# Nineteen weight tiles in the ring instead of seventeen, second weights stored by pairs of row blocks, and a smaller DMA scratch

## The chip, the cores and the metric

The kernel runs on one core of a Trainium2 chip, in one launch. The metric is the device time of an execution in microseconds. The engines are TensorE (PE; its weight loads are PEld), VectorE (DVE), ScalarE (ACT), GpSimd (POOL) and SyncE (SP), which here issues nearly all transfers. Each engine works through its own instructions in order; semaphores hold them until data has come or a buffer is free.

## The reference

Two transformer blocks run over 256 tokens of width 1024, all in fp32. What matters here is the first block's expert layer and the shapes of the rest:

```python
# block 1: a mixer (causal convolution of 31 taps, attention of 8 heads with forget gates, gates), then
def moe_ffn(h, w_router, b_router, w1, b1, w2, b2):      # 32 experts, the best 4 for each token
    logits = hf @ w_router + b_router
    top_v, top_e = lax.top_k(logits, TOP_K)
    gates = softmax(top_v)
    ...
    hc = xi @ w1[e] + b1[e]                              # 1024 -> 2048
    g, u = min(hc[:, :1024], 7), clip(hc[:, 1024:], -7, 7)
    hm = (u + 1) * (g * sigmoid(1.702 * g))
    yb = hm @ w2[e] + b2[e]                              # 1024 -> 1024
    y = sum over a token's four experts of gate * yb
# block 2: mixer(0), a feed-forward layer of 22 x 128 hidden columns, mixer(1),
#          then a second expert layer: 8 experts, 11 x 128 hidden columns, the best 2 for each token
```

The first expert layer alone reads 32 x (8 + 4) MiB of weights; the whole kernel reads 694 MB.

## The kernel before, in words

The stages of one execution, with their places in the profile: the first mixer (0 to 255 us), the first expert layer (255 to 1220), a normalisation and mixer(0) (1220 to 1437), the feed-forward (1437 to 1630), mixer(1) (1630 to 1825) and the second expert layer (1825 to the end).

**Weights and the ring.** Every weight tile is 128 partitions of 2048 fp32 numbers (1 MiB). `load` (line 245, its transfer is issued on line 247) takes the next tile of a ring and has SyncE start the transfer. A pool of seven tiles, `ring`, lives through the whole kernel. While a stage has room left, `more_ring` names a second pool and an order: a letter "m" is a tile of that pool, a letter "r" one of the seven. In the first expert layer the order is `RING1` with 17 letters, ten "m" and seven "r"; in the second it is "rrrrrrrm", eight. A tile is written again when the products that read it are done, so the load of one tile waits on the products that used the tile 17 loads before.

**The first expert layer.** For each of 32 experts eight tiles of first weights (`in_wei`, a block of 128 rows of 8 KB each) and four of second weights (`in_weo`, two blocks of 128 rows of 4 KB each) are loaded, in that order. The number of tokens that an expert has room for is fixed by `SIZE1` (s: 32, m: 64, b: 128). TensorE gathers the tokens (line 911), multiplies by the first weights (line 957 for s, line 963 for m and b; PSUM names `h`), turns and activates, multiplies by the second weights (line 998; PSUM name `s`) and scatters the result (line 1028) into `xres`. The first expert's 12 tiles and the first `PRE1` = 4 tiles of the second are asked for ahead of the layer's other work, in a fixed order (`ordered=True`, lines 882 to 894); the other loads stand in the loop over the experts, the ring alone holds them back. From the third expert on the weights' place is read from a register, since the router has decided which expert comes.

**The other stages** multiply in split form: a weight tile is cut into a high half `wh` (ScalarE cast, line 326) and a low half `wl` (VectorE difference, line 329), and TensorE multiplies three times (`mm3`, lines 306 to 308). A scheduler sets the engines' orders there. The second weights of these stages (`in_w2out`, `in_wf2`, `in_wm2`) come in tiles of two 128-row blocks as well (lines 1208 and 1807). The convolution of the first mixer is a row of VectorE steps `acv` (line 482). In the second expert layer ScalarE also scales hidden products (`ms`, line 1676) and casts them (`mhh`, line 1682).

GpSimd starts a few small loads itself: expert biases (lines 885 to 892) and rows of the normalisations (line 1170).

Of the kernel before, what the change touches and what calls it, by code (L numbers as in the profile page):

```python
# [19 lines left out]
P = 128  # L20
# [14 lines left out]

RING1 = "mmrmrmrmrmrmrmrmm"
PRE1 = 4
NE2, CAP2 = 8, 128
# [29 lines left out]
def _const_parts():  # L68
# [6 lines left out]
    iota = np.broadcast_to(np.arange(S, dtype=np.float32), (P, S))  # L75
    i64 = np.arange(CAP1, dtype=np.float32)
    iota2 = np.broadcast_to(np.concatenate([i64, i64, i64 + CAP1, i64 + CAP1]), (P, S))
    tril32 = (i[:, None] > i[None, :NE1]).astype(np.float32)
# [9 lines left out]
    def first(n, fixed):  # L88
        e = np.zeros((P, 1 + n), np.float32)
        for i in range(fixed):  # L90
# [7 lines left out]
    z = [("ident", ident), ("ones", ones), ("sel4", sel4)]  # L98
    a = [("tri", tri), ("stro", np.concatenate([stri, ones], 1)), ("iota", iota), ("iota2", iota2),
         ("tril32", tril32), ("icol", icol), ("slot", slot), ("first1", first(NE1, FIX1)), ("first2", first(NE2, 1)), ("sel", sel), ("route1", routing(NE1, RANK1, np.array(ROOM1))),  # L100
# [35 lines left out]
def prep(inp):  # L136
# [27 lines left out]
    a["x"] = f("x")[0]  # L164

    def ws(w, cw):
        K, N = w.shape
        return np.ascontiguousarray(w.reshape(K // P, P, N // cw, cw).transpose(2, 1, 0, 3).reshape(N // cw, P, -1))
# [15 lines left out]
    a["bei0"] = np.ascontiguousarray(f("b_exp_in")[0, 0].reshape(2, 8, P).transpose(2, 1, 0).reshape(P, 16))  # L184
    a["weo"] = f("w_exp_out")[0]
    a["beo"] = f("b_exp_out")[0]
    for l in range(2):
        w = f("w_in_2")[l]
        s = np.cumsum([0, 512, 128, 128, 256, 256, 512, 512, 512, 2048])
        qa, ka, va, qr, kr, vr, gf, gb, gl = (w[:, s[i]:s[i + 1]] for i in range(9))  # L190
        allc = np.concatenate([qa[:, QPERM], ka, kr, qr, gf, gb, gl], 1)
        a[f"w2in{l}"] = ws(allc[:, :32 * P], 256)
        a[f"w2in{l}t"] = ws(allc[:, 32 * P:], 128)
        vv = np.concatenate([va, vr], 1).reshape(8, P, 640).transpose(1, 0, 2)
        a[f"w2v{l}"] = np.ascontiguousarray(vv.reshape(P, 8 * 640))
        a[f"w2oa{l}"] = ws(f("w_o_attn_2")[l][QPERM], 512)
        a[f"w2or{l}"] = ws(f("w_o_ret_2")[l], 512)
        a[f"w2out{l}"] = f("w_out_2")[l]
    w1, w3 = f("ffn_w1_2")[0].reshape(8, P, 22, P), f("ffn_w3_2")[0].reshape(8, P, 22, P)
    a["wf13"] = np.ascontiguousarray(np.stack([w1, w3], 3).transpose(2, 1, 0, 3, 4).reshape(22, P, CH))  # L200
    a["wf2"] = f("ffn_w2_2")[0]
    m1, m3 = (f(n)[0].reshape(8, 8, P, FT2, P) for n in ("moe_w1_2", "moe_w3_2"))
    a["wm13"] = np.ascontiguousarray(np.stack([m1, m3], 4).transpose(0, 3, 2, 1, 4, 5).reshape(8, FT2, P, CH))
    a["wm2"] = f("moe_w2_2")[0]
    wr2 = np.zeros((P, 8, 32), np.float32)
# [10 lines left out]
def two_blocks(ctx: ExitStack, tc: tile.TileContext, I, out, dbg=None, upto=None):  # L216
# [13 lines left out]
    keep = ctx.enter_context(tc.tile_pool(name="keep", bufs=1, reuse_waits="tile"))  # L230
    ring = ctx.enter_context(tc.tile_pool(name="ring", bufs=7))
    more_ring, turn = [], [-1]
# [3 lines left out]
    def ring_tile():  # L236
        turn[0] += 1
        if more_ring:
            pool, order = more_ring
            i = turn[0] % len(order)  # L240
            if order[i] == "m":
                return pool.tile([P, CH], F32, tag=f"w{i}", name=nm("w"), bufs=1)
        return ring.tile([P, CH], F32, tag="w", name=nm("w"))

    def load(src, n=CH, ordered=False):
# [634 lines left out]
    with ExitStack() as pb:  # L880
# [11 lines left out]
        G.dma_start(b10, I["bei0"])  # L892
        first_w += [load(I["weo"][0, k * 256:(k + 1) * 256, :].rearrange("(k p) d -> p k d", p=P), ordered=True) for k in range(4)]
        second_w = [load(I["wei"][1, k * P:(k + 1) * P, :], ordered=True) for k in range(PRE1)]
# [203 lines left out]
        for p in range(NE1):  # L1098
            while (p, CHK1[p][-1]) not in ready or group[2] and p in [g[0] for g in group[1]]:
                gather_on(8)  # L1100
            if p == 0:
                w1, w2 = first_w1, (lambda kk: first_w[8 + kk])
            elif p < FIX1:
                w1 = lambda k: second_w[k] if k < PRE1 else load(I["wei"][p, k * P:(k + 1) * P, :])
                w2 = lambda kk: load(I["weo"][p, kk * 256:(kk + 1) * 256, :].rearrange("(k p) d -> p k d", p=P))
# [17 lines left out]
        with tc.tile_pool(name="xtra", bufs=1, reuse_waits="tile") as xk:  # L1123
            cur = xk.tile([P, 1], F32, name="cur")
            V.memset(cur, 0.0)
            with tc.For_i(0, n_extra, 1):
# [14 lines left out]
                def xload(src):  # L1141
# [5 lines left out]
                expert1(lambda k: xload(I["wei"][bass.ds(er, 1), k * P:(k + 1) * P, :].rearrange("a p c -> p (a c)")),  # L1147
                        lambda kk: xload(I["weo"][bass.ds(er, 1), kk * 256:(kk + 1) * 256, :].rearrange("a (k p) d -> p (a k) d", p=P)),
                        [xg], lambda: [([pe[:, 0:1], pe[:, 1:2]], KA["slot"][:, 0:1], [ge[:, 0:1], ge[:, 1:2]])], b1)
# [9 lines left out]
    with ExitStack() as pc:  # L1159
# [45 lines left out]
        def token_major(wsrc, n, src, accs):  # L1205

            def chunk(c):
                return split(load(wsrc[c * 256:(c + 1) * 256, :].rearrange("(k p) d -> p k d", p=P)), D)

# [322 lines left out]
        def moe2():  # L1532
            with ExitStack() as pe_:
# [8 lines left out]

                more_ring[:] = [wk, "rrrrrrrm"]
                g2t = wk.tile([P, 2, NE2], F32, name="g2t")
# [260 lines left out]
                def weights(er):  # L1805
                    return (lambda f: I["wm13"][bass.ds(er, 1), f].rearrange("a p c -> p (a c)"),
                            lambda f, n: I["wm2"][bass.ds(er, 1), f * P:(f + n) * P, :].rearrange("a (k p) d -> p (a k) d", p=P))

# [11 lines left out]
                def expert(p):  # L1820
                    if p == 0:
                        w13 = lambda f: I["wm13"][0, f]
                        w2 = lambda f, n: I["wm2"][0, f * P:(f + n) * P, :].rearrange("(k p) d -> p k d", p=P)
                    else:
                        w13, w2 = weights(nc.sync.value_load(route2.oi[0:1, p:p + 1], min_val=0, max_val=NE2 - 1))
# [99 lines left out]
```

## Time and profile before

| | us |
|---|---|
| median of three runs | 2271.04 |
| lowest and highest | 2269.56 and 2273.24 |
| the profiled execution | 2276.11 |
| its span in the trace | 2274.2 |
| mean granted TensorE clock in it | 0.958 |

The profile shows one execution. Its first section gives each engine's busy time; the second cuts the span into 40 slices of 56.9 us and gives tenths of busy time, granted clock and DMA share, and what the transfers moved in GB/s. The trace of the same execution was asked for windows by stage, for what ended the waits of an engine, for single lines and for timelines. TensorE is at 93% over the whole span, and the slices show that its holes and the highest transfer rates lie in the same places, from about 255 to 1220 us.

### The profile page before, as it was taken

Reading aid. Unit: us, or ns where it says so; the run is one execution under the profiler, and the core shown is the slowest. Engines: PE = TensorE matmul, PEld = TensorE weight load, DVE = VectorE, ACT = ScalarE, POOL = GpSimd, SP = SyncE. Lnnn points to the kernel's source line nnn. Section 1 sums busy time; section 2 is a strip of 40 time slices with the busy share of each in tenths; the row PEclk is TensorE's granted clock in tenths of the full one; section 3 lists DMA queues with packets and bytes.
Section 4 is the critical chain, followed back from the end, with each engine's and each line's share of the span. In section 5 each row is a group of like instructions: output and inputs, shape, how many; then the busy total and the mean of one; then the engine's idle time right before and its main releaser. Section 6 shows DMA issues by size and latency. Waiting matters only on the chain. (4 is left out here: it accounts for less than half of the span.)

```text
span 2274.2 us, 34778 instructions
## 1 busy us (share of the span) xinstructions
PE 2105.5 (93%) x13882; PEld 1411.1 (62%) x13882; DVE 1122.5 (49%) x2050; ACT 782.0 (34%) x1317; POOL 30.4 (1%) x45
## 2 busy tenths in 40 slices
PE   6999998799999999989897999999999989999996
PEld 4888533233333333333334989899898978878883
DVE  3986333223233142322234666655566676348882
ACT  3355211111111011111102675444466465336761
POOL 0000000000000000000000000000000000000000
PEclk8999999989999999999897999999999989999998
DMA  9756789999999999999999524455543456989884
GB/s 392 287 201 269 251 326 414 417 416 382 418 416 416 418 403 416 417 418 417 417 417 361 184 103 167 168 187 190 182 164 112 169 188 245 383 323 379 317 332 185
DMA packets 122632, 697.57 MB, mean 307 GB/s; under 512 B 11120, under 2 KB 11648, under 8 KB 63936
## 3 DMA queue, kind: packets, MB, share of 16 engines
q1 hardware_dynamic: 121120, 690.54, 77.6%
q0 software_dynamic: 1344, 4.73, 0.6%
q8 instruction: 112, 1.84, 0.3%
q14 instruction: 56, 0.46, 0.1%
HBM read 694.18 MB, written 1.05 MB: 306 GB/s over the span
## 5 line engine op out<-in xcount | busy, mean ns | idle before, releaser
L329 DVE TENSOR_TENSOR wl<-w,wh 128x1024 fp32r<-128x1024 f32 (+1 forms) x393 | 472.2, 1217 | 187.3 <-ACT wh L326 184.4
L326 ACT CAST wh<-w 128x1024 fp32r<-128x1024 f32 (+1 forms) x393 | 404.8, 1045 | 232.3 <-PE acc L307 66.9
L963 PE MATMUL h<-w,xg 128*64 128x512 f32 x1280 | 295.5, 602 | 11.6 <-DMA w<-in_wei 11.6
L998 PE MATMUL s<-w,hm 128*64 128x512 f32 (+1 forms) x1088 | 257.0, 665 | 23.5 <-DVE xres L1031 12.8
L963 PEld LDWEIGHTS h<-w,xg 128*64 128x64 f32 x1280 | 90.3, 138 | 196.7 <-issue 160.4
L974 ACT COPY hs<-h 128x512 f32<-128x512 f32 x34 | 19.9, 586 | 377.5 <-PE h L963 275.2
L998 PEld LDWEIGHTS s<-w,hm 128*64 128x64 f32 (+1 forms) x1088 | 63.2, 134 | 139.3 <-issue 98.4
L307 PE MATMUL acc<-xTl,wh 128*128 128x256 f32 x528 | 149.2, 283 | 0.0
L306 PE MATMUL acc<-xTh,wh 128*128 128x256 f32 x528 | 149.2, 283 | 0.0
L308 PE MATMUL acc<-xTh,wl 128*128 128x256 f32 x528 | 149.0, 282 | 0.0
L974 DVE COPY hs<-h 128x512 f32<-128x512 f32 x20 | 13.8, 691 | 239.9 <-PE h L963 239.9
L911 PEld LDWEIGHTS t<-oh,xh 128*128 128x128 f32 x512 | 72.5, 213 | 82.9 <-ACT xg L912 32.1
L957 PE MATMUL h<-w,xg 128*32 128x512 f32 x896 | 107.8, 613 | 5.0 <-DMA w<-in_wei 5.0
L912 ACT ACTIVATE xg<-t,modc,a 128x128 f32<-128x128 f32 (+3 forms) x128 | 55.1, 440 | 161.1 <-PE t L911 136.5
L1011 DVE TENSOR_TENSOR ys<-s,g2s 128x512 f32<-128x512 f32 x34 | 23.5, 691 | 167.8 <-PE s L998 167.7
L911 PE MATMUL t<-oh,xh 128*128 128x128 f32 (+3 forms) x512 | 88.7, 314 | 15.0 <-ACT xg L912 8.2
L308 PEld LDWEIGHTS acc<-xTh,wl 128*128 128x128 f32 x528 | 99.3, 188 | 2.8 <-issue 2.3
L306 PEld LDWEIGHTS acc<-xTh,wh 128*128 128x128 f32 x528 | 99.3, 188 | 2.8 <-issue 2.2
L307 PEld LDWEIGHTS acc<-xTl,wh 128*128 128x128 f32 x528 | 99.3, 188 | 0.9 <-issue 0.3
L306 PE MATMUL f<-fxh,wh 128*128 128x256 f32 x352 | 99.2, 282 | 0.7 <-ACT fxh L1238 0.7
L307 PE MATMUL f<-fxl,wh 128*128 128x256 f32 x352 | 99.1, 282 | 0.0
L308 PE MATMUL f<-fxh,wl 128*128 128x256 f32 x352 | 98.8, 281 | 0.0
(551 smaller groups left out, 4255.5 us busy)
## 6 DMA issues: line engine op xcount, KB each, us to landing
w<-in_wei SPq DMA_DIRECT2D x256, 1024.0 KB, 19.7
w<-in_weo SPq DMA_DIRECT2D x128, 1024.0 KB, 19.9
w<-in_wm SPq DMA_DIRECT2D x128, 1024.0 KB, 6.8
w<-in_wf SPq DMA_DIRECT2D x33, 1024.0 KB, 4.8
w<-in_w2in SPq DMA_DIRECT2D x32, 1024.0 KB, 4.9
w<-in_wada SPq DMA_DIRECT2D x24, 1024.0 KB, 9.6
w<-in_win SPq DMA_DIRECT2D x16, 1024.0 KB, 9.0
w<-in_w2out SPq DMA_DIRECT2D x8, 1024.0 KB, 4.8
```

What stands on the lines that cost most here:

```text
L306: T.matmul(o, l[0], r[0], start=start, stop=False)
L307: T.matmul(o, l[0], r[1], start=False, stop=False)
L308: return T.matmul(o, l[1], r[0], start=False, stop=stop)
L326: A.copy(wh[:, :m], w[:, o:o + m])
L329: V.tensor_sub(wl[:, :m], w[:, o:o + m], wh[:, :m])
L911: T.matmul(pt[:, 0:n], xh2[:, tt, k * P:(k + 1) * P], oh[:, tt, 0:n], start=tt == 0, stop=tt == 1)
L912: taken.append(A.activation(xg[:, k, 0:n], pt[:, 0:n], AF.Identity, bias=sh2[:, k:k + 1], scale=a2[:, k:k + 1]))
L957: T.matmul(ph[0][0][32 * q:32 * q + 32, :].rearrange("p (i c) -> p i c", i=4), chunks[0][:, k], w5[:, q % 2, q // 2], start=k == 0, stop=k ...
L963: T.matmul(p[j][64 * gu:64 * gu + 64, :], xs[:, k], w[:, gu * D + j * 512:gu * D + j * 512 + 512], start=k == 0, stop=k == 7)
L974: (A.copy if j == 0 else V.tensor_copy)(hs[:, j], p[j])
L998: T.matmul(p[r, :], hm[:, kk * 2 + k], w[:, k * D + hf * 512:k * D + hf * 512 + 512], start=kk == 0 and (small or k == 0), stop=kk == 3 an ...
L1011: V.tensor_tensor(ys, p, g2s, op=ALU.mult)
```

## The change

`RING1` has 19 letters instead of 17: "mm", then "r" and "m" in turn, then "m" again, with eight "r" and eleven "m"; the pool `ring` has eight tiles instead of seven in the whole kernel. `PRE1` is 6. The order of the second expert layer has one "r" more, nine letters. The room comes from two places: a constant table `iota2` of 256 columns is dropped, and the program is built with a dynamic DMA scratch of 2048 bytes for a partition instead of 16384, which is the size that holds without the argument.

The second weights (`weo`, `w2out`, `wf2`, `wm2`) are rearranged on the host (`two`): of each pair of 128-row blocks, row p of the first block and row p of the second now lie one behind the other, so that a tile is one block of 128 rows of 8 KB (`pair_of`). The tile in SBUF holds the same numbers in the same places as before.

```diff
-RING1 = "mmrmrmrmrmrmrmrmm"
-PRE1 = 4
+RING1 = "mmrmrmrmrmrmrmrmrmm"
+PRE1 = 6
...
-    i64 = np.arange(CAP1, dtype=np.float32)
-    iota2 = np.broadcast_to(np.concatenate([i64, i64, i64 + CAP1, i64 + CAP1]), (P, S))
...
+    def two(w):
+        *e, K, N = w.shape
+        n = K // P // 2
+        even = w[..., :n * 2 * P, :].reshape(*e, n, 2, P, N).swapaxes(-3, -2).reshape(*e, -1)
+        return np.concatenate([even, w[..., n * 2 * P:, :].reshape(*e, -1)], -1)
...
-    a["weo"] = f("w_exp_out")[0]
+    a["weo"] = two(f("w_exp_out")[0])
...
-    ring = ctx.enter_context(tc.tile_pool(name="ring", bufs=7))
+    ring = ctx.enter_context(tc.tile_pool(name="ring", bufs=8))
...
+    def pair_of(src, c, n=2):
+
+        o = c * 2 * P * D
+        return src[..., o:o + n * P * D].rearrange("(p c) -> p c" if len(src.shape) == 1 else "a (p c) -> p (a c)", p=P)
...
-        first_w += [load(I["weo"][0, k * 256:(k + 1) * 256, :].rearrange("(k p) d -> p k d", p=P), ordered=True) for k in range(4)]
+        first_w += [load(pair_of(I["weo"][0], k), ordered=True) for k in range(4)]
         second_w = [load(I["wei"][1, k * P:(k + 1) * P, :], ordered=True) for k in range(PRE1)]
...
-                w2 = lambda kk: load(I["weo"][bass.ds(er, 1), kk * 256:(kk + 1) * 256, :].rearrange("a (k p) d -> p (a k) d", p=P))
+                w2 = lambda kk: load(pair_of(I["weo"][bass.ds(er, 1)], kk))
...
-                more_ring[:] = [wk, "rrrrrrrm"]
+                more_ring[:] = [wk, "rrrrrrrrm"]
...
-    nc = _bacc.Bacc("TRN2", target_bir_lowering=False, num_devices=1)
+    nc = _bacc.Bacc("TRN2", target_bir_lowering=False, num_devices=1, dynamic_dma_scratch_size=2048)
```

The same edit as that of `weo` is made for `w2out`, `wf2` and `wm2`. All lines of the kernel's body lie nine lines further down after the change.

SyncE's order at the end of the first expert's loads and the start of the second's, before (w_311 is the last tile of the first expert, w_312 to w_315 are the second expert's early ones, w_380 to w_382 its next ones from the loop over the experts):

```order
L247 DMA w_311_2483<-in_weo 128x2x1024
L247 DMA w_312_2485<-in_wei 128x2048
L247 DMA w_313_2487<-in_wei 128x2048
L247 DMA w_314_2489<-in_wei 128x2048
L247 DMA w_315_2491<-in_wei 128x2048
L247 DMA w_380_2788<-in_wei 128x2048
L247 DMA w_381_2794<-in_wei 128x2048
L247 DMA w_382_2800<-in_wei 128x2048
```

The same place on SyncE after:

```order
L256 DMA w_311_2483<-in_weo 128x2048
L256 DMA w_312_2485<-in_wei 128x2048
L256 DMA w_313_2487<-in_wei 128x2048
L256 DMA w_314_2489<-in_wei 128x2048
L256 DMA w_315_2491<-in_wei 128x2048
L256 DMA w_316_2493<-in_wei 128x2048
L256 DMA w_317_2495<-in_wei 128x2048
L256 DMA w_382_2800<-in_wei 128x2048
```

The place of no load has moved: the fifth and sixth of the second expert are now early ones, and w_311 is one block of long rows.

VectorE in the first mixer, before (`wl` are low halves of weights, `acv` convolution steps):

```order
L521 COPY fT<-tr_848 128x256
L482 SCALAR_TENSOR_TENSOR acv<-apad,cols,acv 128x256
L329 TENSOR_TENSOR wl_572<-w_569,wh_571 128x1024
L329 TENSOR_TENSOR wl_576<-w_569,wh_575 128x1024
L482 SCALAR_TENSOR_TENSOR acv<-apad,cols,acv 128x256 x19
L329 TENSOR_TENSOR wl_645<-w_642,wh_644 128x1024
```

VectorE at the same place after:

```order
L530 COPY fT<-tr_848 128x256
L338 TENSOR_TENSOR wl_572<-w_569,wh_571 128x1024
L338 TENSOR_TENSOR wl_576<-w_569,wh_575 128x1024
L491 SCALAR_TENSOR_TENSOR acv<-apad,cols,acv 128x256 x19
L338 TENSOR_TENSOR wl_645<-w_642,wh_644 128x1024
L338 TENSOR_TENSOR wl_649<-w_642,wh_648 128x1024
```

The two differences of w_569 stand ahead of a convolution step that they stood behind, and the next two stand together.

ScalarE early in the second expert layer, before (`ms` and `mhh` are hidden products, `wh` high halves of weights):

```order
L1676 ACTIVATE ms_16879<-b_16741 128x256
L326 CAST wh_16890<-w_16888 128x1024
L326 CAST wh_16894<-w_16888 128x1024
L1676 ACTIVATE ms_16956<-b_16810 128x256
L1682 CAST mhh_16739<-t_16882 128x256
L326 CAST wh_16924<-w_16922 128x1024
L326 CAST wh_16928<-w_16922 128x1024
```

ScalarE at the same place after:

```order
L1685 ACTIVATE ms_16879<-b_16741 128x256
L335 CAST wh_16890<-w_16888 128x1024
L335 CAST wh_16894<-w_16888 128x1024
L335 CAST wh_16924<-w_16922 128x1024
L1691 CAST mhh_16739<-t_16882 128x256
L335 CAST wh_16928<-w_16922 128x1024
L1685 ACTIVATE ms_16956<-b_16810 128x256
```

One cast of the next tile now stands ahead of the cast of hidden products, and `ms_16956` stands behind both. In the first expert layer no engine's order differs.

## Rows read from the trace of the kernel before

**Rows 1.** The page: span, TensorE, rate by slice, packets, software queue, one group.

```profile
span 2274.2 us, 34778 instructions
...
PE 2105.5 (93%) x13882; PEld 1411.1 (62%) x13882; DVE 1122.5 (49%) x2050; ACT 782.0 (34%) x1317; POOL 30.4 (1%) x45
...
GB/s 392 287 201 269 251 326 414 417 416 382 418 416 416 418 403 416 417 418 417 417 417 361 184 103 167 168 187 190 182 164 112 169 188 245 383 323 379 317 332 185
DMA packets 122632, 697.57 MB, mean 307 GB/s; under 512 B 11120, under 2 KB 11648, under 8 KB 63936
...
q0 software_dynamic: 1344, 4.73, 0.6%
...
L329 DVE TENSOR_TENSOR wl<-w,wh 128x1024 fp32r<-128x1024 f32 (+1 forms) x393 | 472.2, 1217 | 187.3 <-ACT wh L326 184.4
```

**Rows 2.** Windows: length, PE, PEld, DVE, ACT, POOL busy, clock, DMA share, GB/s.

```profile
60.00:255.00 195.00, 189.48 (x1438) 159.83 (x1437) 144.38 (x329) 86.89 (x136) 3.60 (x6) 0.98 0.64 247
255.00:366.00 111.00, 104.08 (x534) 45.05 (x537) 36.18 (x105) 19.18 (x43) 0.00 (x0) 0.94 0.88 329
366.00:496.00 130.00, 112.45 (x624) 41.52 (x616) 31.48 (x69) 16.00 (x33) 0.00 (x0) 0.97 1.02 417
...
549.00:1220.00 671.00, 610.97 (x3088) 229.71 (x3086) 196.74 (x422) 77.81 (x167) 0.00 (x0) 0.95 1.02 416
...
1900.00:2060.00 160.00, 154.07 (x1579) 128.68 (x1578) 78.33 (x129) 58.35 (x118) 0.00 (x0) 0.98 0.86 337
2060.00:2260.00 200.00, 193.02 (x1322) 161.31 (x1321) 146.03 (x178) 116.31 (x166) 0.00 (x0) 0.99 0.83 312
```

**Rows 3.** SyncE's waits from 200, 366 and 496: total us, times, longest.

```profile
SPq L247 <- PE h L963: 47.5, 15, 14.8
...
SPq L247 <- DMA w<-in_wei: 39.9, 23, 2.2
...
SPq L247 <- PE s L998: 32.4, 7, 14.9
```

**Rows 4.** Line 247 at 329.5, at 515 and from 1100 to 1210 us.

```profile
DMA to landing us min/median/max: 4.8/4.8/4.8
...
DMA to landing us min/median/max: 4.9/4.9/4.9
...
DMA to landing us min/median/max: 16.7/19.9/20.1
```

**Rows 5.** TensorE's waits for tiles, 255 to 1220 us.

```profile
PE h L963 <- DMA w<-in_wei: 11.6, 20, 1.4
...
PE h L957 <- DMA w<-in_wei: 5.0, 6, 1.4
PE s L998 <- DMA w<-in_weo: 1.5, 1, 1.5
```

**Rows 6.** TensorE's timeline: start, length, instructions, idle before and its releaser.

```profile
425.50 1.94 PE L963 MATMUL h<-w,xg 128*64 128x512 f32 x8 [1.42 <-DMA w<-in_wei]
427.99 1.94 PE L963 MATMUL h<-w,xg 128*64 128x512 f32 x8 [0.55 <-DMA w<-in_wei]
...
1106.23 1.94 PE L963 MATMUL h<-w,xg 128*64 128x512 f32 x8 [0.55 <-DMA w<-in_wei]
...
1214.45 5.34 PE L998 MATMUL s<-w,hm 128*32 128x512 f32 x32 [1.41 <-DVE hm L986]
```

**Rows 7.** Windows: two with first weights landing, then two with second weights.

```profile
1127.00:1141.00 14.00, 14.00 (x42) 6.03 (x42) 0.19 (x1) 1.51 (x4) 0.00 (x0) 0.55 1.01 420
1157.00:1171.00 14.00, 11.43 (x53) 4.29 (x50) 6.87 (x16) 1.90 (x4) 0.00 (x0) 1.00 1.01 418
...
1145.00:1150.00 5.00, 5.00 (x25) 1.71 (x25) 1.41 (x2) 0.00 (x0) 0.00 (x0) 1.00 1.02 406
...
1205.00:1210.00 5.00, 4.40 (x44) 1.02 (x36) 0.00 (x0) 0.47 (x1) 0.00 (x0) 1.00 1.03 410
```

More of the change, by code (lines that the diff above doesn't have):

```diff
@@ L98, in _const_parts @@
     z = [("ident", ident), ("ones", ones), ("sel4", sel4)]
-    a = [("tri", tri), ("stro", np.concatenate([stri, ones], 1)), ("iota", iota), ("iota2", iota2),
+    a = [("tri", tri), ("stro", np.concatenate([stri, ones], 1)), ("iota", iota),
          ("tril32", tril32), ("icol", icol), ("slot", slot), ("first1", first(NE1, FIX1)), ("first2", first(NE2, 1)), ("sel", sel), ("route1", routing(NE1, RANK1, np.array(ROOM1))),
@@ L197, in prep @@
         a[f"w2or{l}"] = ws(f("w_o_ret_2")[l], 512)
-        a[f"w2out{l}"] = f("w_out_2")[l]
+        a[f"w2out{l}"] = two(f("w_out_2")[l])
     w1, w3 = f("ffn_w1_2")[0].reshape(8, P, 22, P), f("ffn_w3_2")[0].reshape(8, P, 22, P)
     a["wf13"] = np.ascontiguousarray(np.stack([w1, w3], 3).transpose(2, 1, 0, 3, 4).reshape(22, P, CH))
-    a["wf2"] = f("ffn_w2_2")[0]
+    a["wf2"] = two(f("ffn_w2_2")[0])
     m1, m3 = (f(n)[0].reshape(8, 8, P, FT2, P) for n in ("moe_w1_2", "moe_w3_2"))
     a["wm13"] = np.ascontiguousarray(np.stack([m1, m3], 4).transpose(0, 3, 2, 1, 4, 5).reshape(8, FT2, P, CH))
-    a["wm2"] = f("moe_w2_2")[0]
+    a["wm2"] = two(f("moe_w2_2")[0])
     wr2 = np.zeros((P, 8, 32), np.float32)
@@ L1104, in two_blocks @@
                 w1 = lambda k: second_w[k] if k < PRE1 else load(I["wei"][p, k * P:(k + 1) * P, :])
-                w2 = lambda kk: load(I["weo"][p, kk * 256:(kk + 1) * 256, :].rearrange("(k p) d -> p k d", p=P))
+                w2 = lambda kk: load(pair_of(I["weo"][p], kk))
             else:
@@ L1147, in two_blocks @@
                 expert1(lambda k: xload(I["wei"][bass.ds(er, 1), k * P:(k + 1) * P, :].rearrange("a p c -> p (a c)")),
-                        lambda kk: xload(I["weo"][bass.ds(er, 1), kk * 256:(kk + 1) * 256, :].rearrange("a (k p) d -> p (a k) d", p=P)),
+                        lambda kk: xload(pair_of(I["weo"][bass.ds(er, 1)], kk)),
                         [xg], lambda: [([pe[:, 0:1], pe[:, 1:2]], KA["slot"][:, 0:1], [ge[:, 0:1], ge[:, 1:2]])], b1)
@@ L1207, in chunk @@
             def chunk(c):
-                return split(load(wsrc[c * 256:(c + 1) * 256, :].rearrange("(k p) d -> p k d", p=P)), D)
+                return split(load(pair_of(wsrc, c)), D)
             def products(w, c, tt, halves=(0, 1)):
@@ L1806, in weights @@
                     return (lambda f: I["wm13"][bass.ds(er, 1), f].rearrange("a p c -> p (a c)"),
-                            lambda f, n: I["wm2"][bass.ds(er, 1), f * P:(f + n) * P, :].rearrange("a (k p) d -> p (a k) d", p=P))
+                            lambda f, n: pair_of(I["wm2"][bass.ds(er, 1)], f // 2, n))
                 def columns(t, p):
@@ L1822, in expert @@
                         w13 = lambda f: I["wm13"][0, f]
-                        w2 = lambda f, n: I["wm2"][0, f * P:(f + n) * P, :].rearrange("(k p) d -> p k d", p=P)
+                        w2 = lambda f, n: pair_of(I["wm2"][0], f // 2, n)
                     else:
```

## The prediction

> **What bounds the kernel now.** I read the page first [rows 1], then the windows stage by stage [rows 2], because the 93% of TensorE is a mean over stages with different limits. TensorE works through 189 of 195 us before the first expert layer and 347 of the last 360 us, in the second expert layer, while DMA is at 0.64 to 0.86 of its time. Those stages are TensorE's (the mixers and the feed-forward between 1240 and 1825 move under 200 GB/s and belong with them). The first expert layer, 255 to 1220 us, is different: DMA stands at 1.02 of its time with 416 to 417 GB/s, while TensorE has 17.5 of 130 us free, then 60 of 671.
>
> So I followed the weight loads there. One expert is 12 tiles of 1 MiB. Up to 330 us the rate is only 329 GB/s: SyncE is holding loads back until TensorE gives ring tiles free [rows 3]. The load at 329.51 us lands 4.8 us after its issue, and one between 1100 and 1210 takes 19.9 us [rows 4]. The first found the queue empty; the others land behind a full one, eight tiles with their own (8 x 2.49 us = 19.9). From there SyncE waits for the loads themselves (39.9 us in 23 waits from 366 to 496), with one break: a wait of 14.9 us for TensorE's second weights, after which a load at 515 us again lands in 4.9 us [rows 3, 4]. The GB/s line shows it as 382 among slices of 416 to 418, and a smaller hole of 403 at 796 to 853 us [rows 1].
>
> Is this train of loads on the path? TensorE waits for tiles of it 27 times, 18.1 us together [rows 5]; in the timeline at 425 us it takes a tile every 2.49 us and works on it 1.94 [rows 6]. Between such places it is late and uses up its ring, but it meets the train again: at 1103 to 1116 us it still waits 0.55 us a tile. What makes the train earlier up to there therefore passes on to the end of the stage, as long as TensorE still catches up with it.
>
> **Two more tiles (and two more early loads).** A load can be issued when the tile that lay 17 tiles before is free; now the one 19 before. The limit by the ring ends at the load of 329.51 us; from there the train is a chain of equal landings. With two tiles more the same release lets the train run two tiles further on: 2 x 2.49 = 5.0 us. If TensorE's own pace were the step it would be 2 x 1.94 = 3.9; if the limit only moved to another place, 0. I take 5.0, because from that load on the landings set the step and TensorE's 1.94 no longer does. The two early loads w_316 and w_317 take the seventy-fifth and seventy-sixth place in SyncE's order, where the same two blocks' loads stood as w_380 and w_381; they need no other release than the ring's, and no queue is passed.
>
> The break at 496 to 515: the slice at 382 instead of 417 GB/s lost 0.084 x 56.9 = 4.8 us. Train and TensorE both come there earlier (TensorE had met the train at 425 us and takes its gain over), so the break stays but for the two tiles further that the loads may run: two tiles of second weights take TensorE 2.7 us by the timeline's 5.34 us for four [rows 6]. I take -2.5, ends 0 and -4.8. The hole at 796 (0.034 x 56.9 = 1.9 us): the train has moved and TensorE has not yet met it again after the widest expert, so the same two tiles are eaten by the shift; 0, ends 0 and -1.9.
>
> **Second weights by pairs.** Tiles of both kinds hold 1 MiB. In stretches where only one kind lands, the first weights run at 420 and 418 GB/s and the second at 406 and 410 [rows 7], which is 1.0486 MB / 419 GB/s = 2.50 us against 1.0486 / 408 = 2.57, or 0.07 us a tile. The first weights' tile is 128 rows of 8 KB on both sides, the second's 256 rows of 4 KB, and after the change it has the first's form in every respect. So the second weights take the first's rate. From 330 us to the last waits near 1116 there are 786 us at 8 x 2.50 + 4 x 2.57 = 30.3 us an expert, 26 experts; the first and the last of them count only in part, so I take 24, or 96 tiles: 96 x 0.07 = -6.7 us. Ends: 0, if the rate depends on something else than the row's length, and -7.8 for the 112 tiles from 330 us to the stage's end.
>
> The Trainium skill, "DMA: Bandwidth & Descriptors", section "Why small descriptors are slow (HBM only)", gives a fixed overhead of about three cycles for each packet, on beats of 32 B. By it, as an estimate, 4 KB costs 131 cycles and 8 KB 259, so that pairs save 1.2% or 0.03 us a tile, 2.9 us for 96 tiles in place of 6.7. The rows show 2.7% between the two kinds, over twice that. The same page, section "Where 436 GB/s comes from", puts the limit of transfers out of HBM at about 358 GB/s for a core; by that the row's length could change nothing, and this term would be 0. The rows at 406 and 420 lie above it, so that limit does not bind here.
>
> The pairs in the later stages (w_out, feed-forward, second expert layer) shorten transfers that lie beside TensorE at 0.98 to 0.99 of its time: 0, bound 40 tiles x 0.07 = -2.8.
>
> **What else moves.** The last mixer steps before the experts: VectorE's order puts a pair of `wl` halves ahead of a convolution step instead of behind it; TensorE has 5.5 us free there in 195 [rows 2], so it can be worth between -5.5 and +5.5; I take 0, since both orders issue the same instructions. Second expert layer: the ring grows from eight to nine and ScalarE takes some casts `wh` ahead of a copy `mhh`. TensorE has 5.9 + 7.0 us free from 1900 to 2260 [rows 2], so -12.9 is the one end, and I take as much the other way; value 0, because ScalarE's order is the same again from some twenty rows further on to the end. The dropped table makes one load 128 KB smaller, hidden beside the first stage. The smaller DMA scratch concerns GpSimd's queue: 1344 packets, 0.6% of 2274 us, i.e. 13.6 us of transfer in all if nothing lay beside it [rows 1]. These are 13 small loads, rows and biases, which are issued long before they are used; 0, ends 0 and +13.6.
>
> **Sum.** -5.0 - 2.5 - 6.7 = -14.2, say -14. The profiled execution is 2276.11 (span 2274.2 and 1.9 around it) and would come to 2262; it lies 5.1 above the median of the three runs, so the median goes from 2271.0 to 2257.
>
> **A cap, and the rivals.**
> All of TensorE's waits for the train are 18.1 us [rows 5]. The one clock price beside it: from 1127 to 1141 us the granted clock is 0.55 (that is near the lower of its levels of 1.2 and 2.4 GHz), right behind the stretch in which TensorE waited before each tile, and 42 matmuls took 14.0 us, which at the rate of the later stretch, 53 in 11.43, would be 9.1 [rows 7]: 4.9 us.
>
> A. The forecast: 2251 to 2262, 0.59.
> B. Pairs do nothing, the ring alone acts: -7.5, so 2263.5. For it: both kinds of tile move the same bytes over the same engines, and the second kind's stretches are short (four tiles). Against it: both stretches of each kind agree. 0.14.
> C. TensorE is freed altogether: the train stays ahead everywhere and the clock does not fall: -18.1 - 4.9 = -23, 2248. For it: the last waits are only 0.55 us a tile. Against it: after -14 TensorE has yet to make up some of its own lateness after the wide experts. 0.10.
> D. The change of order costs in the second expert layer, or before the first, what the train gains, some 10 to 18 us out of the bounds of 5.5 and 12.9: within 4.5 us of 2271. For it: VectorE is busy 146 of the last 200 us [rows 2]. Against it: ScalarE's and VectorE's moved instructions are few. 0.11.
> E. Slower, one mechanism: in the second expert layer the ninth tile lets loads and splits run further ahead, and VectorE's in-order queue holds back the products' own steps behind `wl` splits of 1.2 us each (mean, [rows 1]). To end slower by over 4.5 us it must eat 14.2 + 4.5 = 18.7, that is 16 such splits in TensorE's way; at 24 of them the time would be 2286. 0.06.
>
> That the change doesn't do what it says (two more tiles that give no longer distance, because a tile of another kind lies between) is part of D's chance; with the pairs alone it would be 2264.
>
> **How the numbers follow.** 0.2% (4.5 us) is about what a measurement of this kernel can tell from no change. Faster: A, B and C, 0.83. Same: D, 0.11. Slower: E, 0.06. The time is A's, 2257; A's own range is 2251 to 2262. For 8 in 10 the range goes from just below C to just above B and the sums with one unknown at its bad end: 2247 to 2266.
>
> **What would show it.** Packets under 8 KB fall from 63936 by 256 for each paired tile, to about a quarter; stretches with second weights alone run at 418 to 421 GB/s (B would show 407). The early loads w_316 and w_317 are issued right behind w_315. The slices of the first expert layer lose the 382 or bring it nearer to 417. TensorE's waits for tiles fall below 18.1 us, the layer ends near 1206 instead of 1220, and what follows it is as long as before (1054 us) within 3. I'd be wrong if the layer's end moved by under 8 us or by over 20, if the time before or behind it grew (D, E).

## The result, and the profile after

The changed kernel takes 2251.13 us (median of 4 runs, 2249.46 to 2253.18) against 2270.30 before (4 runs of the same job). The ratio is 0.9914, with a 95% interval from 0.9902 to 0.9927: faster by 19.5 us, between 17 and 22. The prediction was 2257 in a range of 2247 to 2266. The direction and the range held; the gain is 1.4 times the 14 us of the sum, and part of it came from a stage that had been put at nothing.

The page of the changed kernel, to be read against [rows 1]; the GB/s line is the rate in 40 slices of 56.3 us:

```profile
span 2251.3 us, 34782 instructions
...
PE 2092.2 (93%) x13882; PEld 1410.2 (63%) x13882; DVE 1121.9 (50%) x2050; ACT 785.1 (35%) x1317; POOL 30.4 (1%) x45
...
GB/s 396 303 203 251 282 323 416 421 421 420 421 421 421 421 407 421 421 421 422 421 421 360 168 104 166 179 190 182 185 162 110 165 187 258 382 313 414 316 333 164
DMA packets 98697, 697.44 MB, mean 310 GB/s; under 512 B 11120, under 2 KB 11648, under 8 KB 16064
```

Packets under 8 KB fell from 63936 to 16064, a quarter. From 394 us on the slices of the first expert layer lie at 420 to 422 (416 to 418 before) but for one of 407, and the one of 382 is gone. TensorE issues the same 13882 matmuls and is busy 13.3 us less.

Two windows for each kernel split the execution at the end of the first expert layer (columns as in [rows 2]; the first window begins with TensorE's first gather, the second is all that follows). Before:

```profile
252.60:1219.80 967.20, 880.31 (x4480) 338.65 (x4480) 284.76 (x640) 120.67 (x261) 0.00 (x0) 0.94 1.00 404
1219.80:2274.20 1054.40, 996.43 (x7688) 884.64 (x7688) 670.33 (x1046) 555.58 (x897) 25.40 (x31) 0.97 0.61 224
```

After:

```profile
252.30:1202.20 949.90, 867.12 (x4480) 336.32 (x4480) 284.69 (x640) 120.85 (x260) 0.00 (x0) 0.96 1.00 411
1202.20:2251.30 1049.10, 995.64 (x7688) 883.60 (x7688) 669.81 (x1047) 558.01 (x897) 25.33 (x31) 0.97 0.60 225
```

So the expert layer is 17.3 us shorter, what follows it 5.3, and the first mixer 0.3. That is 22.9 between the two traces, and 19 to 20 between the medians. The lengths of the last two parts repeat within about 1 us from trace to trace wherever a stage has the same program (a second trace of the kernel before has 967.0 and 1054.5). The first mixer's doesn't: over the fourteen traces of this study it is 247.7 to 252.6 us, also where the first mixer has the same order of instructions, and the two traces above both lie at its long end. The causes below are therefore read from the two repeatable parts.

### The profile page after: what moved, and what is told of

The parts are those of the page before. It is cut to its first block, busy times and chain, and to the rows that moved or that the text cites. A ratio compares the mean times of both kernels' runs of the same rounds, so it can differ in the third digit from the quotient of the medians.

```text
span 2251.3 us, 34782 instructions
## 1 busy us (share of the span) xinstructions
PE 2092.2 (93%) x13882; PEld 1410.2 (63%) x13882; DVE 1121.9 (50%) x2050; ACT 785.1 (35%) x1317; POOL 30.4 (1%) x45
## 2 busy tenths in 40 slices
DMA packets 98697, 697.44 MB, mean 310 GB/s; under 512 B 11120, under 2 KB 11648, under 8 KB 16064
## 3 DMA queue, kind: packets, MB, share of 16 engines
HBM read 694.05 MB, written 1.05 MB: 309 GB/s over the span
## 5 line engine op out<-in xcount | busy, mean ns | idle before, releaser
L1007 PE MATMUL s<-w,hm 128*64 128x512 f32 (+1 forms) x1088 | 250.4, 649 | 21.5 <-DVE xres L1040 12.3
L1020 DVE TENSOR_TENSOR ys<-s,g2s 128x512 f32<-128x512 f32 x34 | 23.5, 691 | 157.7 <-PE s L1007 157.6
## 6 DMA issues: line engine op xcount, KB each, us to landing
w<-in_win SPq DMA_DIRECT2D x16, 1024.0 KB, 10.3
```

The costliest lines, as they stand in the source:

```text
L1007: T.matmul(p[r, :], hm[:, kk * 2 + k], w[:, k * D + hf * 512:k * D + hf * 512 + 512], start=kk == 0 and (small or k == 0), stop=kk == 3 an ...
L1020: V.tensor_tensor(ys, p, g2s, op=ALU.mult)
```

## The experiments

The lengths of the two parts (in us) are read from one trace each, as in the windows above. The difference against before (in us) is worked out from the ratio of the medians and its 95% interval, each run beside runs of the kernel before; the medians of those lie between 2270.2 and 2272.4.

| run | median | against before | expert layer | what follows |
|---|---|---|---|---|
| before (two traces) | 2270.2 to 2272.4 | | 967.2, 967.0 | 1054.4, 1054.5 |
| changed | 2251.13 | -19.5 (-22.2 to -16.6) | 949.9 | 1049.1 |
| e1 ring only | 2257.40 | -14.5 (-18.2 to -10.7) | 956.9 | 1048.6 |
| e2 pairs only | 2262.30 | -10.9 (-14.3 to -7.5) | 958.5 | 1055.1 |
| e3 scratch only | 2273.60 | +1.6 (-0.7 to +4.1) | 967.1 | 1054.5 |
| e4 changed, 8 tiles late | 2256.32 | -16.8 (-20.4 to -12.9) | 950.0 | 1054.6 |
| e5 casts behind | 2251.61 | -21.8 (-25.2 to -18.2) | 950.1 | 1049.4 |
| e6 rows of 2 KB | 2274.65 | +2.7 (+0.7 to +4.8) | 974.0 | 1049.0 |
| e7 fifteen tiles | 2282.00 | +8.0 (+4.8 to +11.1) | 977.2 | 1054.8 |
| e9 both behind | 2254.26 | -17.3 (-20.4 to -14.3) | 950.1 | 1052.9 |
| e10 8 tiles, wl ahead | 2251.67 | -19.3 (-22.3 to -16.1) | 950.3 | 1051.2 |
| e11 ten tiles late | 2249.95 | -22.0 (-25.7 to -18.6) | 950.0 | 1048.3 |
| e12 table kept | 2251.03 | -21.8 (-25.5 to -17.9) | 949.2 | 1048.1 |

**e1, the ring alone.** All of the change but the pairs; the orders of all engines are the changed kernel's.

```diff
-RING1 = "mmrmrmrmrmrmrmrmm"
-PRE1 = 4
+RING1 = "mmrmrmrmrmrmrmrmrmm"
+PRE1 = 6
...
-    ring = ctx.enter_context(tc.tile_pool(name="ring", bufs=7))
+    ring = ctx.enter_context(tc.tile_pool(name="ring", bufs=8))
...
-                more_ring[:] = [wk, "rrrrrrrm"]
+                more_ring[:] = [wk, "rrrrrrrrm"]
```

> Nineteen tiles, six early loads, nine in the second expert layer, small scratch; second weights as before in 4 KB rows. Theory T (the run-ahead of the ring is worth more than predicted, because both holes in the train close as well): the first expert layer ends 9 to 11 us earlier (5.0 at 330 us, 2.5 to 4.4 at the break of 496 to 515, 0 to 1.6 at 796), the stage before 1.1 earlier, so -10 to -12 against before, about 2259. Rival R (ring as predicted, the rest of the -19 comes from the rows and from the later stages): -7.5, about 2263; second-weight stretches at 408 GB/s in both.

The expert layer is 10.3 us shorter and what follows 5.8; second weights still land at their old rate. In the size of the expert layer T holds (9 to 11), but T had left the second place out: more than a third of this kernel's gain lies behind the first expert layer. The tiles and the early loads were moved together, here and in e7; no run tells them apart.

**e2, the pairs alone.** Ring, scratch and table as before; no engine's order differs from before.

```diff
-    a["weo"] = f("w_exp_out")[0]
+    a["weo"] = two(f("w_exp_out")[0])     # and w2out, wf2, wm2; loads by pair_of
```

> Seventeen tiles as before, second weights in pairs (8 KB rows), the same order of every instruction as before. Theory T: second weights land at the first weights' rate (2.49 us a tile, 420 GB/s), which is 0.28 us an expert; but the break at 496 to 515 us stays and eats what was gained up to there, so -4 to -5 against before. If the terms simply add: -6.7. If the rows' length does nothing: 0 and 2.55 us a tile. The second expert layer, the mixers and the feed-forward unchanged within 0.5 us in all three.

Neither number holds. The layer is 8.7 us shorter, more than the 4 to 5 of T and than the 6.7 of plain addition; what follows takes 1055.1 us (before 1054.4), so the pairs of the later stages are worth nothing there, as predicted. Alone the parts give -10.3 and -8.7, together -17.3: they nearly add. The rate behaves as predicted. Windows with nothing but second weights landing, in the pairs alone and in the changed kernel (of before: 406 and 410, [rows 7]):

```profile
1136.50:1145.50 9.00, 7.93 (x38) 3.06 (x36) 4.15 (x11) 1.35 (x3) 0.00 (x0) 1.00 1.02 422
```

```profile
1128.50:1137.50 9.00, 7.93 (x38) 3.00 (x36) 3.98 (x11) 1.35 (x3) 0.00 (x0) 1.00 1.02 422
1158.50:1167.50 9.00, 7.93 (x38) 3.06 (x36) 5.45 (x13) 1.35 (x3) 0.00 (x0) 1.00 1.02 422
```

**e3, the scratch and the dropped table alone.**

```diff
-    nc = _bacc.Bacc("TRN2", target_bir_lowering=False, num_devices=1)
+    nc = _bacc.Bacc("TRN2", target_bir_lowering=False, num_devices=1, dynamic_dma_scratch_size=2048)
```

> Only the small DMA scratch and the dropped table; ring, early loads and rows as before. In the first mixer the engines' orders are those of the changed kernel. Theory T: -1 us (the first mixer ends at 242.4 instead of 243.5 us in the trace, and the train of the first expert layer starts that much earlier), the rest as before. Rival S (the scratch holds GpSimd's loads back or frees something): over 2 us either way, with GpSimd's loads landing later.

The expert layer and what follows have before's length to 0.1 us, so S falls for these two parts. GpSimd's four loads ahead of the expert layer land 5.5 to 9.2 us after their issue (6.3 to 8.8 in the trace of before). T's -1 us isn't seen either; the median lies 1.6 us the other way, and the interval has both signs.

**e4, eight tiles in the second expert layer.** One letter less than in the changed kernel; in that layer all orders are then those of before.

```diff
-                more_ring[:] = [wk, "rrrrrrrrm"]
+                more_ring[:] = [wk, "rrrrrrrm"]
```

> The changed kernel with eight tiles in the second expert layer as before, where every engine's order is then that of before. Theory T (the trace of before had one late tile at 2057 us that is not in every run): like the changed kernel, -18 to -19 against before. Rival M (the ninth tile is what took 5.8 us out of the second expert layer in the trace): -13 to -14 against before, and the wait of 3.4 us for wl at the start of the sixth expert comes back in its trace, with a low clock behind it.

M holds: what follows takes 1054.6 us again, 5.5 more than in the changed kernel, while the first expert layer keeps its 950.0. TensorE's wait for `wl` is back.

The place is the start of the fifth expert of that layer (the expectation calls it the sixth). TensorE and VectorE there before (start, length, engine, line, instruction, idle before and its releaser):

```profile
2053.20 0.38 PE L306 MATMUL b<-wh,mxh 128*128 128x256 f32 x1
2056.98 0.58 PE L307 MATMUL b<-wl,mxh 128*128 128x256 f32 x1 [3.40 <-DVE wl L329]
```

```profile
2051.79 0.69 DVE L1660 TENSOR_TENSOR my0l<-b,my0h 128x512 fp32r<-128x512 f32 x1 [1.15 <-ACT my0h L1659]
2053.07 2.73 DVE L1668 SCALAR_TENSOR_TENSOR xres<-b,gp,xres 128x512 f32<-128x512 f32 x4 [0.59 <-PE b L1665]
2055.71 4.62 DVE L329 TENSOR_TENSOR wl<-w,wh 128x1024 fp32r<-128x1024 f32 x4
```

And after, TensorE and VectorE:

```profile
2034.85 0.39 PE L315 MATMUL b<-wh,mxh 128*128 128x256 f32 x1
2035.08 0.27 PE L316 MATMUL b<-wl,mxh 128*128 128x256 f32 x1
```

```profile
2032.37 2.35 DVE L338 TENSOR_TENSOR wl<-w,wh 128x1024 fp32r<-128x1024 f32 x2
2034.63 0.69 DVE L1669 TENSOR_TENSOR my0l<-b,my0h 128x512 fp32r<-128x512 f32 x1
2035.23 1.22 DVE L338 TENSOR_TENSOR wl<-w,wh 128x1024 fp32r<-128x1024 f32 x1
2036.37 2.72 DVE L1677 SCALAR_TENSOR_TENSOR xres<-b,gp,xres 128x512 f32<-128x512 f32 x4
```

Before, the differences `wl` stand behind four additions into `xres`, and these wait for the scatter products of the expert before. After, three `wl` stand ahead of the additions, two of them ahead of `my0l` too. TensorE's matmuls behind the wait take 0.41 us instead of 0.28, at a granted clock of 0.72 over 12 us (after: 1.00):

```profile
2052.00:2064.00 12.00, 8.60 (x52) 7.61 (x51) 10.06 (x11) 6.38 (x7) 0.00 (x0) 0.72 1.01 425
```

```profile
2034.00:2046.00 12.00, 11.81 (x93) 10.94 (x94) 12.00 (x14) 8.61 (x10) 0.00 (x0) 1.00 1.01 422
```

Two things differ there, the ninth tile and the order; three more runs take them apart. The order differs in more places than the two shown with the change: from 1820 to 2100 us (times of before) ScalarE, VectorE and TensorE all have instructions in other places. One example, ScalarE before and after, some 15 us behind the wait: the scaling `ms` that stood ahead of the cast `mhh` now stands behind it and a cast `wh`.

```profile
2070.38 0.39 ACT L1676 ACTIVATE ms<-b 128x256 f32<-128x256 f32 x1 [1.80 <-PE b L308]
2070.66 0.37 ACT L1682 CAST mhh<-t 128x256 fp32r<-128x256 f32 x1
2070.91 3.90 ACT L326 CAST wh<-w 128x1024 fp32r<-128x1024 f32 x4
```

```profile
2047.76 0.38 ACT L1691 CAST mhh<-t 128x256 fp32r<-128x256 f32 x1 [0.61 <-PE t L1689]
2048.03 1.06 ACT L335 CAST wh<-w 128x1024 fp32r<-128x1024 f32 x1
2048.98 0.39 ACT L1685 ACTIVATE ms<-b 128x256 f32<-128x256 f32 x1
```

Up to 2050 us the other orders make no difference: counted by TensorE's matmuls from the end of the first expert layer, the two kernels are level there, and behind the place the gap of 5.3 us no longer changes.

**e5, the casts behind.** The changed kernel, with ScalarE's first casts of the fifth expert held behind the copy `my0h`, where they stood before.

```diff
+                hold[:] = [(spread_copy[:], [])]     # the copy my0h of the expert before
                 run(expert(4))
```

> The changed kernel, nine tiles in the second expert layer, but the casts of the fifth expert's first tile are ordered behind the copy my0h again, as they stood before the change. Theory O (the 5.5 us that the ninth tile took out of the second expert layer come from ScalarE's order, which the scheduler changed): the wait for wl at the start of the fifth expert comes back (2 to 3.4 us) with a low clock behind it, so +3 to +5.5 against the changed kernel, about -14 to -16 against before. Rival T9 (the load that goes out earlier in the ninth tile is enough): like the changed kernel within 1 us, -19 against before.

By the length of what follows, 1049.4 us, O falls. The first casts go out beside the scatter products again, at 2030.82 us, where the changed kernel has them 7 us ahead of these; VectorE still has one `wl` ahead of the additions, and TensorE's longest wait for `wl` there is 0.7 us. That this length hides a loss at the place itself is shown behind e10.

**e9, both behind.** As e5, and `wl` also held behind the last of the four additions.

```diff
+                hold[:] = [(spread_copy[:], spread_add[:])]     # and the last addition into xres
                 run(expert(4))
```

> The changed kernel, nine tiles in the second expert layer, with both engines' orders at the start of the fifth expert as before the change: ScalarE's casts behind my0h and VectorE's differences wl behind the four additions into xres. Theory O2 (the order of VectorE makes the wait of 3.4 us and the low clock behind it; the casts alone were not late enough): what lies behind the first expert layer takes 1053 to 1055 us again, +3.5 to +5.5 against the changed kernel, -14 to -16 against before. Rival T9 (the ninth tile's earlier load): 1049 us, -19 to -20 against before.

With nine tiles, and the casts and `wl` where they stood before, the wait is there to the hundredth, and what follows takes 1052.9 us:

```profile
2033.32 0.38 PE L315 MATMUL b<-wh,mxh 128*128 128x256 f32 x1
2037.10 0.58 PE L316 MATMUL b<-wl,mxh 128*128 128x256 f32 x1 [3.40 <-DVE wl L338]
```

**e10, eight tiles, and `wl` ahead.** As e4, but the four additions of the expert before are emitted late and held behind the first two `wl`.

```diff
-                            V.scalar_tensor_tensor(xres[:, tt, s], po[hf], gate[tt], xres[:, tt, s], op0=ALU.mult, op1=ALU.add)
+                            late.append(one) if defer else one()     # one: the same addition
...
                             w = split(load(w13(f0 + fi)), 256)
+                            while late:
+                                with tc.issue_after(subs[0].ins):
+                                    late.pop(0)()
```

> The changed kernel with eight tiles in the second expert layer, but the four additions into xres of the expert before are ordered behind the first two differences wl of the fifth expert. Theory O2: what lies behind the first expert layer takes 1049 to 1051 us with eight tiles too, -18 to -20 against before. Rival T9: 1054 us as in the run with eight tiles, -15 to -17 against before.

1051.2 us, just outside O2's 1049 to 1051 and far from T9's 1054: eight tiles with two `wl` ahead get 3.4 of the 5.5 us back. A wait of 1.68 us remains, for the third `wl`, now behind the additions.

What follows the expert layer adds up several places, so here is the place alone: the same 107 matmuls of TensorE, by their number from the end of the first expert layer, in before, the changed kernel, e9, e10 and e5 (columns as in [rows 2]; a window also counts the few that reach into it).

```profile
2050.09:2070.06 19.97, 15.88 (x112) 13.98 (x106) 16.11 (x17) 10.94 (x12) 0.00 (x0) 0.83 1.01 424
2032.47:2047.22 14.75, 14.06 (x111) 12.28 (x106) 14.75 (x16) 10.11 (x11) 0.00 (x0) 1.00 1.01 419
2030.22:2050.58 20.36, 16.27 (x111) 14.38 (x106) 15.57 (x17) 11.99 (x13) 0.00 (x0) 0.83 1.02 422
2027.89:2045.00 17.11, 14.31 (x111) 12.21 (x106) 15.68 (x18) 11.98 (x13) 0.00 (x0) 1.00 1.01 424
2029.26:2046.67 17.41, 14.60 (x112) 12.30 (x106) 15.23 (x17) 11.97 (x13) 0.00 (x0) 1.00 1.01 422
```

All six traces with the orders of before take 20.0 to 20.6 us for it (e4: 20.4), all five with the changed ones 14.7 to 14.8. e9 has nine tiles and takes 20.4: the ninth tile by itself is worth nothing here, and the orders are worth all of the 5.2 us. VectorE's part, two `wl` ahead of the additions, is worth 3.3 (e10 against e4). To hold the casts back, and with them two of the three `wl`, costs 2.7 (e5 against the changed kernel), so at the place O was half right. That e5 and e9 end earlier than this says has another cause: at the start of the next expert TensorE waits 1.0 us for a cast and 0.4 us for `wl` before, after and in e10 (here after), and not in e5 and e9, where the same 133 matmuls take 22.4 and 22.1 us instead of 23.8.

```profile
2089.65 0.38 PE L315 MATMUL b<-wh,mxh 128*128 128x256 f32 x1 [1.02 <-ACT wh L335]
2090.39 0.39 PE L316 MATMUL b<-wl,mxh 128*128 128x256 f32 x1 [0.36 <-DVE wl L338]
```

**e6, second weights in rows of 2 KB.** The changed kernel with 512 rows a tile instead of 128.

```diff
-    a["weo"] = two(f("w_exp_out")[0])
+    a["weo"] = half(f("w_exp_out")[0])     # blocks of 128 rows by halves of 512 columns
```

> The changed kernel with the first expert layer's second weights in rows of 2 KB (512 rows a tile) instead of 8 KB (128 rows). Theory T (each row costs a fixed time: 128 rows more cost 0.07 us, so 384 more cost 0.2 us): second weights land every 2.69 us at 390 GB/s, 0.8 us an expert from 330 us on, so +18 to +22 against the changed kernel, about 2270 to 2273, as slow as before or a little slower. Rival (rows below 8 KB cost the same 0.07 us): 2.55 us a tile and +5 to +8 against the changed kernel.

T holds: second weights land every 2.70 us (median of the distances between landings), and the layer is 24.1 us longer than in the changed kernel, a little over what T gave. The window with second weights alone:

```profile
1150.00:1160.00 10.00, 8.93 (x44) 3.40 (x42) 4.14 (x11) 1.34 (x3) 0.00 (x0) 1.00 1.05 402
```

**e7, fifteen tiles.** The kernel before with two tiles fewer; no engine's order differs from before.

```diff
-RING1 = "mmrmrmrmrmrmrmrmm"
-PRE1 = 4
+RING1 = "mmrmrmrmrmrmrmm"
+PRE1 = 2
```

> The kernel before with fifteen tiles and two early loads; every engine's order is that of before. Theory T (two tiles are worth 5.0 us at 330 us and 2 to 5 us more at the two holes of the train): +8 to +12 against before, 2279 to 2282, with holes at 496 to 515 and 796 us that are longer. Rival R (two tiles are worth 7.5 us): +7 to +8. Rival N (two tiles are worth less at this end because TensorE already waits): under +4.

The layer is 10.0 us longer, the mirror of e1's -10.3, so two tiles are worth 10 us around this ring size. The total of +8.0 alone would not tell T from R; the length of the layer does, and N falls.

**e8, before again.**

> The kernel before, unchanged, for a second trace. What lies behind the first expert layer should again take 1054.4 us within 0.5 and TensorE's wait of 3.4 us for wl at about 2057 us should be there again; the first expert layer's end may differ by 2 or 3 us from the first trace's 1219.8, since the median lies 5 us below that execution.

2275.75 us in one run, 967.0 and 1054.5 us for the two parts: as expected, and the base of the statement that these lengths repeat.

**e11, ten tiles in the second expert layer,** in a scratch of 1024 bytes.

```diff
-                more_ring[:] = [wk, "rrrrrrrrm"]
+                more_ring[:] = [wk, "rrrrrrrrmm"]
```

> The changed kernel with ten tiles in the second expert layer instead of nine, in a DMA scratch of 1024 bytes. Theory O2 (the tile itself is worth little there, TensorE is busy 98 of 100): within 1 us of the changed kernel. Rival T9 (each tile more lets the loads go out earlier): 1 to 4 us faster than the changed kernel.

1048.3 us, 0.8 less than with nine: as O2 has it, at the edge of what T9 would give, and within the 1 us by which these lengths repeat.

**e12, the table kept.** The changed kernel with `iota2` put back, in a scratch of 1024 bytes: in the first mixer the orders are those of before.

```diff
-    a = [("tri", tri), ("stro", np.concatenate([stri, ones], 1)), ("iota", iota),
+    a = [("tri", tri), ("stro", np.concatenate([stri, ones], 1)), ("iota", iota), ("iota2", iota2),
```

> The changed kernel with the constant table of 256 columns put back (in the room of a DMA scratch of 1024 bytes): in the first mixer every engine's order is that of before, elsewhere that of the changed kernel. By the parts of the traces the changed kernel should be 22.5 us faster than before; measured are 19.5. Theory A (the new order in the first mixer costs 2 to 3 us there, which the spread of single traces hides): -21 to -23 against before, 2 to 3 us faster than the changed kernel. Rival Z (the order costs nothing; the gap is the spread of the first stage from execution to execution): -18 to -20, like the changed kernel.

-21.8 lies in A's range, with an interval that holds both expectations; its median, 2251.03, is the changed kernel's, which speaks for Z. So the time decides nothing. The traces say more: from TensorE's 400th matmul on, which starts at 71 to 76 us, the rest of the first mixer takes 176.4 to 176.7 us in all fourteen traces, with either order. The spread lies ahead of it, at 72.2 to 76.2 us with the order of before (five traces) and at 71.3 to 75.8 with the changed one (nine). No trace shows the 2 to 3 us of A.

## Why the prediction was right, and where it was not

**The train of loads is the bound of the first expert layer: right.** TensorE's instructions in it and their order did not change, only the loads did, and the layer's length followed in both directions (e1, e2, e6, e7). In all fourteen traces the layer ends between 2.2 and 4.4 us after its last tile has landed (before: 1219.8 and 1216.7 us).

**Two tiles move the train by 5.0 us: right, and seen in the trace.** The last load that waits on the ring ahead of the full train goes out at the same time in both kernels, and two tiles further along. SyncE's timeline at the fourth expert's eight first weights, before and after (start, time over the group, issues in it):

```profile
329.51 13.06 SPq L247 DMA_DIRECT2D w<-in_wei  x7
```

```profile
329.59 10.55 SPq L256 DMA_DIRECT2D w<-in_wei  x5
```

Seven loads of that expert were still to come, now five. Counted from TensorE's first gather, the fourth expert's last tile lands 4.3 us earlier in e1 and 5.6 later in e7.

**The break at 496 to 515 and the hole at 796: mis-sized.** The break's term said -2.5, ends 0 and -4.8. Between these two traces it came to the far end: the tenth expert's twelve landings took 34.98 us before and 30.33 after, 4.65 less, of which 0.28 is the rate. The windows after against [rows 2], with that stretch as the third:

```profile
255.00:366.00 111.00, 104.07 (x532) 44.76 (x536) 36.13 (x105) 18.92 (x43) 0.00 (x0) 0.94 0.90 349
366.00:496.00 130.00, 115.23 (x634) 42.76 (x626) 37.80 (x85) 16.78 (x35) 0.00 (x0) 0.97 1.01 421
496.00:549.00 53.00, 51.55 (x249) 20.41 (x248) 18.56 (x38) 6.69 (x14) 0.00 (x0) 0.88 1.01 420
```

SyncE still waits for TensorE there, 12.2 us at the longest (14.9 before, [rows 3]; the window is 480 to 549 us), but the loads in flight, 20 us of them, now last until it goes on:

```profile
SPq L256 <- PE s L1007: 33.7, 8, 12.2
```

I had priced the two tiles by TensorE's time for them (2.7 us) and not by what they still cover. The hole at 796, put at 0, gave 1.6 (the twentieth expert's landings took 32.50 and 30.60 us). How the loss divides over these places differs from trace to trace (in the second trace of before the break cost 2.7 us, not 4.9, and the layer was as long), so only the whole is firm. Twelve landings that nothing stops take 30.1 us with rows of 4 KB. What the 28 experts from the fifth on take beyond that is 11.7 and 11.4 us in the two traces of before, 11.2 in e3 and 6.4 in e1: some 5 us, where the sum had 2.5. The ring's whole term was 10.3 (e1; 10.0 in e7) instead of 7.5.

**The pairs: the rate right, the count wrong.** 0.07 us a tile was measured (2.56 to 2.49 us). Of the 128 tiles I took 96, up to the last place where TensorE waited before. But the layer ends with its last landing, so every tile behind 330 us counts. With the pairs twelve landings that nothing stops take 29.8 us instead of 30.1, and over the 28 experts from the fifth on that is 28 x 0.3 = 8.4; e2 has 8.7. Nor is the last wait a fixed place: in the second trace of before, as long as the first, TensorE waits for the train in the last expert too:

```profile
1201.07 1.07 PE L957 MATMUL h<-w,xg 128*32 128x512 f32 x8 [1.43 <-DMA w<-in_wei]
1203.55 1.52 PE L957 MATMUL h<-w,xg 128*32 128x512 f32 x8 [1.42 <-DMA w<-in_wei]
```

The far end of this term, -7.8 for 112 tiles, had the right count. The bound for the later stages had not: by the fall in packets (187 x 256, 128 of them in the first expert layer) 59 later tiles became pairs, not 40. e2 shows that nothing hangs on it.

The Trainium skill, "DMA: Bandwidth & Descriptors", section "Why small descriptors are slow (HBM only)", made it an estimated 0.03 us a tile; the trace disagrees, by more than twice.

**The cap was none.** TensorE's waits for the train, 18.1 us before [rows 5], are still 14.1 after:

```profile
PE h L972 <- DMA w<-in_wei: 8.9, 15, 1.6
...
PE h L966 <- DMA w<-in_wei: 5.2, 5, 1.4
```

In the second trace of before they are 23.5, and that layer is as long as in the first. The changed layer is 17.3 us shorter all the same. In the windows above 13.2 of these are TensorE's busy time for the same 4480 matmuls, 880.3 to 867.1, at a granted clock of 0.96 instead of 0.94. I had taken the waits and one stretch at low clock as the most that could be had. The waits are no such bound: the layer ends with the train, however TensorE's lateness is divided into waits and slow stretches.

**The second expert layer: the step that failed.** It was put at 0 "because ScalarE's order is the same again from some twenty rows further on to the end". That reason fails: ScalarE's order differs in many places up to 2077 us (the rows at 2070 and 2048 us above), and VectorE's and TensorE's differ too. I had looked at ScalarE's rows and not at VectorE's, nor asked what the one long wait there, 3.4 us for `wl`, had in front of it in VectorE's queue. e4, e5, e9 and e10 show what came in its place: what follows the expert layer, put at "as long as before (1054 us) within 3", is 5.3 us shorter, all of it at this one place, by the wait and the slow matmuls behind it. The orders do it, VectorE's two `wl` 3.3 us of it, and the ninth tile only in that the scheduler chose these orders with it. It is the mirror of rival E, a split behind other work on VectorE's queue, and before the change it was already there. No part of D's loss came in this layer.

**At nothing, and right:** the pairs of the later stages (e2), the scratch and GpSimd's loads (e3), and the first mixer's order behind its first 76 us (all fourteen traces).

The sum with the measured sizes: -10.3 - 8.7 + 1.7 (the two together are less than their sum) - 5.3 = -22.6; measured by the ratio -19.5, between -22.2 and -16.6. What is left, some 3 us, can only lie in the first mixer, and there in its first 76 us: by subtraction (the median less the two parts and the 1.9 us around the span) it took 247 to 249 us in the median run of before and 250 in that of the changed kernel. By the same subtraction e2 and e7, with before's order there, have 247 and 248, the other kernels with the changed order 248 to 250, and e12, with before's order, 252. So the medians lean towards a cost of the new order, e12 and the traces do not; it stays open.

That the time lies in the forecast's own range of 2251 to 2262, by 0.1 us, is in part luck. The ring, the pairs and the second expert layer each gave more than the sum had, and would have led to about 2248; the first mixer took some 3 us of it back.

## What to carry to other kernels

Where a train of loads is the bound, count its terms over the whole train and price its holes by what is in flight, not by what the waiting engine still does today: the place where they meet moves with the change. Where a change touches a scheduler's room anywhere, go through every engine's queue ahead of each single long wait of the trace; a wait of 3 us can hang on four additions that stand in front by chance. And where a stage's length repeats to 1 us while the whole moves by 5, compare stages.

## What the runs showed of the hardware

A tile of 1 MiB lands every 2.485 us in 128 rows of 8 KB, every 2.558 us in 256 rows of 4 KB and every 2.699 us in 512 rows of 2 KB (medians of the distances between second weights' landings from the fifth expert on, in the changed kernel, before and e6): 0.55 to 0.57 ns for each row more, in both steps, at a DMA share of 1.02 to 1.05 in the windows above. A tile has one size here, so the number of rows and their length can't be told apart. And the first mixer, with the same order and the same data, took 247.7 to 252.3 us in nine traces: the difference arises up to TensorE's 400th matmul, at 71 to 76 us, where TensorE waits for the first loads (9.8 us for `in_wada` in the trace of before); what follows takes 176.4 to 176.7.
